# The mixer's sets: high and low parts of the operand side by side, in pairs of PSUM banks

## The chip, the cores and the metric

One core of one Trainium2 chip runs the whole program. The metric is the device time of one execution in microseconds (us). The engines that matter here are TensorE (PE, matmuls; its weight loads are listed apart as PEld), VectorE (DVE), ScalarE (ACT), GpSimd (POOL) and SyncE (SP, which issues most of the loads).

## The reference

One block of a network on 512 positions of width 1024, all in float32: a feed-forward layer (FFN), a mixer, a second FFN, and a last norm.

```
x = x + 0.5 * swiglu(rmsnorm(x), ffn1_w_gu, ffn1_w_down)
x = x + hybrid_mixer(rmsnorm(x), w_in, ...)
x = x + 0.5 * swiglu(rmsnorm(x), ffn2_w_gu, ffn2_w_down)
return rmsnorm(x)

hybrid_mixer(h):
  cb, cc, cu, q, k, v, g_lr, r, ga, gb = split(h @ w_in)
  y_conv = (cb * causal_short_conv(cc * cu)) @ w_out_conv
  log_a  = log_sigmoid(g_lr @ gate_w_up + gate_b) / 16
  o      = chunked gated linear attention of q, k, v, log_a     (4 heads, chunks of 64)
  y_gla  = (rmsnorm(o) * silu(r)) @ w_out_gla
  return (sigmoid(ga) * y_conv + sigmoid(gb) * y_gla) @ w_o
```

The product h @ w_in has a depth of 1024 and more than 8000 columns; it is the mixer's largest piece of work, and the change lies in it.

## The kernel before

**Precision.** Every float32 operand of a matmul is used as a high part (rounded to the matmul's format) and a low part (what the rounding left). A product of weights w and activations a is three matmuls into the same PSUM bank: high w by high a, high w by low a, low w by high a. The high part of a weight tile `wh` is cast on ScalarE (L382), the low part `wl` is the difference, on VectorE (L383), both 128x1024. Three buffers of each are in turn, and the parts are made two steps ahead of their use. Raw weights arrive in tiles `f` by DMAs of SyncE's queue.

**Sets.** Much of the work is done in sets, by a seven-product scheme for 2x2 blocks: the depth is halved, the 512 positions are halved, and two blocks of 256 output columns stand against the two depth halves. In place of eight block products seven are computed, with sums of weight blocks (on VectorE, L367, and by accumulating DMAs on GpSimd's queue, L357) and sums of activation blocks. The products are named m1, p2, q6, p5, q7, p4, p3. One set is 512 output columns by 512 positions at depth 1024, and one product is depth 512 (four tiles, k) by 256 columns (two tiles, e) by 256 positions. The products accumulate into three banks: "b" takes m1, q6, q7 and p4 in turn, with copies of m1, q6 and q7 taken out on ScalarE in between; "a" takes p2; "c" takes p5 and then p3. The quarters of the output are read out of PSUM on VectorE with a kept copy added: p2 + m1, -(c) - q7, c + q6; the last quarter is -b after p4.

**Two forms of a set.** `Set.run` (L563 on) takes an operand whose high and low parts are two tiles. Each (k, e) of a product is three matmuls of 256 positions (all at L577). `run_joint` (L586) takes an operand in which, for each k, 256 high and 256 low values stand side by side. In m1, q6, q7 and p4 it issues the same three matmuls (L607). In p2, p5 and p3 it writes a pair of banks, one bank for each e: one matmul of 512 (L599) multiplies the high weights by high and low part at once, so the main sum comes to stand in the left half of the bank and the cross term in the right half, and one matmul of 256 (L601) adds low weights by high part to the right half. Whoever reads such a bank adds both halves. Before the change the FFNs' sets use the joint form, and the mixer's sets the other.

**The banks.** PSUM has eight banks. Two are the auxiliary ones (`AUX`). The other six are a pool of six single banks (`MM`), or, after `open_banks(True)`, a pool of two single ones and a pool of two pairs (`MM2`). The FFN opens the pairs ahead of its sets and closes them after.

**The mixer's order.** First q and k of the heads by plain products (two heads in a group, then four products `mm_single`, L410 to L412), with `gates(0)` among them. Then v's set (`Tall`, L672 on): the same seven products with the roles exchanged, so that the activations are the stationary operand and 512 weight columns the moving one (L693); it uses two banks for each of "a", "b", "c". Then twelve sets: ga, gb, ga, gb, four of the convolution, two of cb, two of r. The order of products of consecutive sets is woven together by `order`, so that m1 and p2 of the next set come between q7, p4 and p3 of the one before. The steps of the attention are hooks that run after certain products: for each head `gates` (L1171), `decays` (L1186 to L1198), `scale` (L1203), `scores` (L1219), `state`, `output` and `squares`. Head 1's gates come after set 0, head 2's in set 3, head 3's in set 6. `conv_done`, `cb_done` and `act_done` read a set's quarters out of PSUM; `quarter` (L1409) does it for the last two.

**What orders the work.** TensorE takes the products in the order of the plan. Outside the last stage of the program, a planner at compile time places each engine's instructions by the order of the code and by its own reckoning of what is ready; each engine then works through its queue in that order. Pools hand a buffer out again once its last reader is through.

`Operands` makes the summed and split activations of each product when they are needed, two products ahead at the latest: `sum` (L635 to L642) on VectorE, then the cast on ScalarE (L665) and the difference on VectorE (L666), both of 128x1024. In the joint layout it does that in two halves (L658, L659).

Of the kernel before, what the change touches and what calls it, by code (L numbers as in the profile page):

```python
# [12 lines left out]
ALU = mybir.AluOpType  # L13
ENG = mybir.EngineType

P = 128
S = 512
# [62 lines left out]
HW = 256  # L80
# [138 lines left out]
def block_kernel(ctx: ExitStack, tc: tile.TileContext, xT, vecs, gf, gup, wgl, wts, out):  # L219
    nc = tc.nc  # L220
# [8 lines left out]
    def open_banks(pairs):  # L229

        if "ps" in banks_of:
            banks_of["stack"].close()
        banks_of["stack"] = ExitStack()
        banks_of["n"] = banks_of.get("n", 0) + 1
        banks_of["ps"] = banks_of["stack"].enter_context(
            tc.tile_pool(name=f"ps{banks_of['n']}", bufs=2 if pairs else 6,
                         space=bass.MemoryType.PSUM, reuse_waits="tile"))
        if pairs:
            banks_of["pairs"] = banks_of["stack"].enter_context(
                tc.tile_pool(name=f"pp{banks_of['n']}", bufs=2,  # L240
                             space=bass.MemoryType.PSUM, reuse_waits="tile"))
# [16 lines left out]
    def tile_of(pool, shape, dtype=F32):  # L258
        cnt[0] += 1
        return pools[pool].tile(shape, dtype, tag=pool, name=f"{pool}{cnt[0]}")  # L260

    def T(dtype=F32):
        return tile_of("tp", [P, S], dtype)

    def MM():
        cnt[0] += 1
        return banks_of["ps"].tile([P, S], F32, tag="mm", name=f"mm{cnt[0]}")

    def MM2():
        cnt[0] += 1  # L270
        return banks_of["pairs"].tile([P, 2, S], F32, tag="mm2", name=f"mm{cnt[0]}")
# [275 lines left out]
    def mul(out_, a, b, eng=None):  # L547
        (eng or nc.vector).tensor_tensor(out=out_, in0=a, in1=b, op=ALU.mult)  # L548
# [123 lines left out]
    class Tall:  # L672
# [7 lines left out]
        def run(self, p, s):  # L680
            b = {"p2": "a", "p5": "c", "p3": "c"}.get(p, "b")
            fresh = b not in self.bank
            if fresh:
                self.bank[b] = [MM(), MM()]
            bh, bl = self.group.get(p)
            h, l = W.take()
            for i in range(2):
                k = 2 * s + i
                wh, wl = (a[:, 512 * i : 512 * (i + 1)] for a in (h, l))
                for e in range(2):  # L690
                    c = slice(k * HW + e * P, k * HW + (e + 1) * P)
                    for n, (aa, ww) in enumerate(((bh, wh), (bh, wl), (bl, wh))):
                        nc.tensor.matmul(self.bank[b][e], aa[:, c], ww,  # L693
                                         start=fresh and i == 0 and n == 0,
                                         stop=k == 3 and n == 2, skip_group_check=True)
            if s == 1:
                self.done(p, self.bank[b])

    def run_sets(make, ahead=2, hooks={}, tall=None):


        at = W.taken
        seq = []
        while STEPS[at + len(seq)][1] is not None:
            seq.append(STEPS[at + len(seq)])
        sets = {n: None for n, _ in seq if n not in TALL}
        number = {n: i for i, n in enumerate(sets)}
        for n, i in number.items():
            sets[n] = make(i)
        for i, (n, p) in enumerate(seq):  # L710
            for n_, p_ in seq[i : i + ahead + 1]:
                (tall if n_ in TALL else sets[n_]).group.make(p_)
            if n in TALL:
                tall.run(p, TALL[n])
                at = ("tall", TALL[n], p)
            else:
                sets[n].run(p)
                at = (number[n], p)
            for f in hooks.get(at, ()):
                f()  # L720
# [325 lines left out]
    def mixer(norm, nxt):  # L1046
# [21 lines left out]
        def G_tile(i, dtype=F32):  # L1068
# [13 lines left out]
            out=maskf, in_=maskf, pattern=[[1, P]], compare_op=ALU.is_ge, fill=0.0,  # L1082
# [13 lines left out]
        for i in range(2):  # L1096
# [3 lines left out]
                                    in1=gl_w[i][:, :, 0, :RANK].bitcast(F32), op=ALU.subtract)  # L1100
# [3 lines left out]
        for i in range(6):  # L1104
# [3 lines left out]
                                in1=gup_w[R2 : 2 * R2].bitcast(F32), op=ALU.subtract)  # L1108
# [18 lines left out]
        def evac_k(h, o):  # L1127
# [7 lines left out]
                                in1=glr[2 * R2 : R3].bitcast(F32), op=ALU.subtract)  # L1135
# [14 lines left out]
                        in1=row, op0=ALU.mult, op1=ALU.mult)  # L1150
            return X[:, 4 * j : 4 * j + 4, l * HW : (l + 1) * HW]

        xo = Operands(normed)


        def chunks(t):
# [187 lines left out]
        def pair(t):  # L1344
            return t.rearrange("p (e t) -> p e t", t=HW)

        def half(l):
            return slice(l * HW, (l + 1) * HW)
# [19 lines left out]
        def finish_late():  # L1368
            while late:
                late.pop(0)()  # L1370

        def conv_done(i):
            def done(s, p):
                bank, v = s.bank, s.v
                u = Y[i][:, :, 2:]
                if p == "p2":
                    s.t1 = T()
                    nc.vector.tensor_tensor(out=s.t1, in0=bank["a"], in1=v["m1"], op=ALU.add)
                if p == "q7":
                    s.u2 = T()  # L1380
                    nc.vector.scalar_tensor_tensor(out=s.u2, in0=bank["c"], scalar=-1.0,
                                                   in1=v["q7"], op0=ALU.mult, op1=ALU.subtract)
                if p == "p4":
                    nc.vector.scalar_tensor_tensor(
                        out=u[:, :, half(0)], in0=pair(bank["b"]), scalar=-1.0, in1=pair(s.t1),
                        op0=ALU.mult, op1=ALU.mult)
                if p == "p3":
                    t2 = T()
                    nc.vector.tensor_tensor(out=t2, in0=bank["c"], in1=v["q6"], op=ALU.add)
                    mul(u[:, :, half(1)], pair(s.u2), pair(t2))  # L1390
                    late.append(lambda: convolve(i))
            return done
# [16 lines left out]
        def quarter(s, p):  # L1409

            bank, v = s.bank, s.v
            if p not in ("p2", "q7", "p3"):
                return None
            t = T()
            if p == "q7":
                nc.vector.scalar_tensor_tensor(out=t, in0=bank["c"], scalar=-1.0, in1=v["q7"],
                                               op0=ALU.mult, op1=ALU.subtract)
            else:
                nc.vector.tensor_tensor(out=t, in0=bank["a" if p == "p2" else "c"],
                                        in1=v["m1" if p == "p2" else "q6"], op=ALU.add)  # L1420
            return t

        def act_done(func, use):
# [32 lines left out]
        def make(n):  # L1456
# [7 lines left out]

            return Set(xo, done)

        run_sets(make, hooks=hooks, tall=Tall(xo, v_done))
        finish_late()


# [10 lines left out]
        def gate(name, d):  # L1481
            t = T()
            nc.sync.dma_start(t, gates_d[name][d])
            nc.scalar.activation(t, t, AF.Sigmoid)
            return t
# [9 lines left out]
        for d in range(KD):  # L1495
            t = gate("ga", d)
# [12 lines left out]
        for d in range(KD):  # L1509
            t = gate("gb", d)  # L1510
# [87 lines left out]
```

## Time and profile before

| | us |
|---|---|
| median of three runs | 1190.02 (1189.88 to 1190.07) |
| the profiled execution | 1189.97 |
| its span, first to last instruction | 1188.3 |
| TensorE busy in the span | 1177.6 |
| VectorE busy | 900.4 |
| ScalarE busy | 606.5 |
| v's set, about | 391 to 437 |
| the mixer's twelve sets, about | 437 to 707 |

A row of instructions gives start and duration in us, the engine, the line of the kernel, the operation, out<-in by the program's names, the shape, and how many neighbouring instructions were merged into the row; in brackets stands the idle time of the engine before it and whose work ended that. Rows of matmuls overlap, since the next starts before the last has drained; so the distance between starts, not the duration, is what a matmul takes up of TensorE's time.

### The profile page before, as it was taken

The page shows a single profiled execution, that of the slowest core. Times are in us where ns is not written, and L with a number is a line of the kernel's source. Part 1 is how long each engine was busy: PE and PEld are TensorE (multiplying, and loading weights), DVE is VectorE, ACT ScalarE, POOL GpSimd, SP SyncE. Part 2 cuts the span into 40 slices and gives each one's busy share as a digit, 9 for nine tenths or more (in the row PEclk, how much of TensorE's full clock was granted, in tenths as well). Part 3 has the DMA queues.
Part 4 walks back from the last instruction along what each step waited for, and adds up shares of the span by engine and source line. Part 5 has one row for each costly group of instructions (what it writes and reads, how often), then busy time and mean ns, then how long its engine had stood idle before and what let it go on. Part 6 is the DMA issues. An engine that isn't in the chain of part 4 may idle for free. (4 is left out here: it accounts for less than half of the span.)

```text
span 1188.3 us, 18713 instructions
## 1 busy us (share of the span) xinstructions
PE 1177.6 (99%) x7546; PEld 1071.7 (90%) x7546; DVE 900.4 (76%) x1107; ACT 606.5 (51%) x759; POOL 111.3 (9%) x149
## 2 busy tenths in 40 slices
PE   9999999999999999999999999999999999999997
PEld 8899999999988889999999998888889999998886
DVE  7987676989797976677787795455598767785686
ACT  6564555545452847464654564334355554572353
POOL 0011111011110110111010100100001111100100
PEclk9999999999999999999999999999999999999999
DMA  9478787656481776877567766602547777763431
GB/s 350 96 195 186 185 182 192 176 125 164 95 301 60 171 194 175 217 181 199 137 160 163 184 189 192 211 3 98 194 97 189 175 181 182 187 172 116 92 93 71
DMA packets 59335, 193.93 MB, mean 163 GB/s; under 512 B 6672, under 2 KB 10896, under 8 KB 59248
## 3 DMA queue, kind: packets, MB, share of 16 engines
q1 hardware_dynamic: 36912, 124.27, 30.7%
q0 software_dynamic: 17696, 63.97, 29.4%
q10 hardware_dynamic: 4640, 4.49, 1.2%
q8 instruction: 59, 0.97, 0.3%
q14 instruction: 28, 0.23, 0.1%
HBM read 124.55 MB, written 8.39 MB: 112 GB/s over the span
## 5 line engine op out<-in xcount | busy, mean ns | idle before, releaser
L382 ACT CAST wh<-f 128x1024 fp32r<-128x1024 f32 (+1 forms) x331 | 345.9, 1047 | 433.3 <-PE mm L577 123.9
L383 DVE TENSOR_TENSOR wl<-f,wh 128x1024 fp32r<-128x1024 f32 (+1 forms) x331 | 402.3, 1218 | 154.0 <-ACT wh L382 147.1
L577 PE MATMUL mm<-op,wh 128*128 128x256 f32 x1792 | 325.3, 284 | 0.0
L577 PEld LDWEIGHTS mm<-op,wh 128*128 128x128 f32 x1792 | 279.6, 191 | 0.9
L577 PE MATMUL mm<-op,wl 128*128 128x256 f32 x896 | 254.3, 284 | 0.7 <-DVE wl L383 0.7
L607 PE MATMUL mm<-op,wh 128*128 128x256 f32 x1152 | 209.6, 283 | 0.4 <-DVE tp L548 0.4
L357 POOL DMA_DIRECT2D f<-f x114 | 98.3, 863 | 922.4 <-DVE wl L383 489.5
L607 PEld LDWEIGHTS mm<-op,wh 128*128 128x128 f32 x1152 | 179.1, 191 | 2.3 <-issue 0.8
L577 PEld LDWEIGHTS mm<-op,wl 128*128 128x128 f32 x896 | 171.4, 191 | 1.2 <-DVE wl L383 1.1
L607 PE MATMUL mm<-op,wl 128*128 128x256 f32 x576 | 163.0, 283 | 0.0
L599 PE MATMUL mm<-op,wh 128*128 128x512 f32 x432 | 154.4, 398 | 0.0
L601 PE MATMUL mm<-op,wl 128*128 128x256 f32 x432 | 121.3, 281 | 0.0
L410 PE MATMUL mm<-op,wh 128*128 128x512 f32 x292 | 113.7, 389 | 0.0
L412 PE MATMUL mm<-op,wl 128*128 128x512 f32 x292 | 113.6, 389 | 0.0
L411 PE MATMUL mm<-op,wh 128*128 128x512 f32 x292 | 113.6, 389 | 0.0
L607 PEld LDWEIGHTS mm<-op,wl 128*128 128x128 f32 x576 | 110.2, 191 | 0.0
L599 PEld LDWEIGHTS mm<-op,wh 128*128 128x128 f32 x432 | 81.3, 188 | 18.2
L601 PEld LDWEIGHTS mm<-op,wl 128*128 128x128 f32 x432 | 81.7, 189 | 0.0
L410 PEld LDWEIGHTS mm<-op,wh 128*128 128x128 f32 x292 | 54.8, 188 | 11.5 <-issue 0.2
L411 PEld LDWEIGHTS mm<-op,wh 128*128 128x128 f32 x292 | 54.8, 188 | 11.4
L412 PEld LDWEIGHTS mm<-op,wl 128*128 128x128 f32 x292 | 54.8, 188 | 11.4
L434 PE MATMUL mm<-op,wh 128*128 128x512 f32 x256 | 63.8, 391 | 0.0
(266 smaller groups left out, 1455.8 us busy)
## 6 DMA issues: line engine op xcount, KB each, us to landing
f<-wts SPq DMA_DIRECT2D x219, 512.0 KB, 4.4
f<-f POOLq DMA_DIRECT2D x114, 512.0 KB, 4.9
X<-xT SPq DMA_DIRECT2D x8, 256.0 KB, 5.2
xs<-X POOLq DMA_DIRECT2D x8, 256.0 KB, 4.6
ga<-tp ACTq DMA_DIRECT2D x8, 256.0 KB, 5.1
gb<-tp ACTq DMA_DIRECT2D x8, 256.0 KB, 4.5
tp<-ga SPq DMA_DIRECT2D x8, 256.0 KB, 6.1
tp<-gb SPq DMA_DIRECT2D x8, 256.0 KB, 2.7
```

The lines of the kernel that those rows point to most:

```text
L357: nc.gpsimd.dma_start(out_, a, accum_op=ALU.add)
L382: nc.scalar.copy(h[:, :w], raw[:, :w])
L383: nc.vector.tensor_tensor(out=l[:, :w], in0=raw[:, :w], in1=h[:, :w].bitcast(F32), op=ALU.subtract)
L410: nc.tensor.matmul(o, wh, ah, start=first, stop=False)
L411: nc.tensor.matmul(o, wh, al, start=False, stop=False)
L412: nc.tensor.matmul(o, wl, ah, start=False, stop=last)
L434: nc.tensor.matmul(o[c], w[:, s : s + P], a[k], start=k == 0 and j == 0, stop=k == kt - 1 and j == 2)
L577: nc.tensor.matmul(to, ww[:, s], aa[:, t], start=fresh and k == 0 and e == 0 and j == 0, stop=k == 3 and j == 2, skip_group_check=True)
L599: nc.tensor.matmul(o[:, e], h[:, s], a, start=fresh and k == 0, stop=False, skip_group_check=True)
L601: nc.tensor.matmul(o[:, e, HW:], l[:, s], a[:, :HW], start=False, stop=k == 3, skip_group_check=True)
L607: nc.tensor.matmul(to, ww[:, s], aa, start=fresh and k == 0 and e == 0 and j == 0, stop=k == 3 and j == 2, skip_group_check=True)
```

## The change

The mixer's operand `xo` is made in the joint layout, so the mixer's twelve sets run through `run_joint`: p2, p5 and p3 become 512-wide and 256-wide matmuls into pairs of banks. The pairs are opened ahead of v's set and closed after the last set. v's set takes its stationary 128 columns, high and low, from the new layout, and takes "b" and "c" as pairs of banks and "a" as two single ones. `quarter` reads the left halves with the kept copy and then adds (or, for q7, subtracts) the right halves in a second VectorE instruction, and `conv_done` now calls `quarter` in place of its own three copies of that code.

```diff
         def run(self, p, s):
             b = {"p2": "a", "p5": "c", "p3": "c"}.get(p, "b")
             fresh = b not in self.bank
-            if fresh:
+            if fresh and b == "a":
                 self.bank[b] = [MM(), MM()]
-            bh, bl = self.group.get(p)
+            elif fresh:
+                two_banks = MM2()
+                self.bank[b] = [two_banks[:, e] for e in range(2)]
+            parts = self.group.get(p)
             h, l = W.take()
             for i in range(2):
                 k = 2 * s + i
                 wh, wl = (a[:, 512 * i : 512 * (i + 1)] for a in (h, l))
                 for e in range(2):
-                    c = slice(k * HW + e * P, k * HW + (e + 1) * P)
+                    bh, bl = (parts[k // 2][:, k % 2 * S + o : k % 2 * S + o + P]
+                              for o in (e * P, HW + e * P))
                     for n, (aa, ww) in enumerate(((bh, wh), (bh, wl), (bl, wh))):
-                        nc.tensor.matmul(self.bank[b][e], aa[:, c], ww,
+                        nc.tensor.matmul(self.bank[b][e], aa, ww,
...
-        xo = Operands(normed)
+        xo = Operands(normed, joint=True)
...
                 if p == "p2":
-                    s.t1 = T()
-                    nc.vector.tensor_tensor(out=s.t1, in0=bank["a"], in1=v["m1"], op=ALU.add)
+                    s.t1 = quarter(s, p)
                 if p == "q7":
-                    s.u2 = T()
-                    nc.vector.scalar_tensor_tensor(out=s.u2, in0=bank["c"], scalar=-1.0,
-                                                   in1=v["q7"], op0=ALU.mult, op1=ALU.subtract)
+                    s.u2 = quarter(s, p)
...
                 if p == "p3":
-                    t2 = T()
-                    nc.vector.tensor_tensor(out=t2, in0=bank["c"], in1=v["q6"], op=ALU.add)
+                    t2 = quarter(s, p)
...
             t = T()
+            bank = bank["a" if p == "p2" else "c"]
+            main, cross = bank[:, :, :HW], bank[:, :, HW:]
             if p == "q7":
-                nc.vector.scalar_tensor_tensor(out=t, in0=bank["c"], scalar=-1.0, in1=v["q7"],
-                                               op0=ALU.mult, op1=ALU.subtract)
+                nc.vector.scalar_tensor_tensor(out=pair(t), in0=main, scalar=-1.0,
+                                               in1=pair(v["q7"]), op0=ALU.mult, op1=ALU.subtract)
             else:
-                nc.vector.tensor_tensor(out=t, in0=bank["a" if p == "p2" else "c"],
-                                        in1=v["m1" if p == "p2" else "q6"], op=ALU.add)
+                nc.vector.tensor_tensor(out=pair(t), in0=main,
+                                        in1=pair(v["m1" if p == "p2" else "q6"]), op=ALU.add)
+            nc.vector.tensor_tensor(out=pair(t), in0=pair(t), in1=cross,
+                                    op=ALU.subtract if p == "q7" else ALU.add)
             return t
...
+        open_banks(True)
         run_sets(make, hooks=hooks, tall=Tall(xo, v_done))
+        open_banks(False)
         finish_late()
```

## The prediction

> **What bounds the kernel now.** I read the page's busy table first, then the busy time by stage, then TensorE's own waits, and last the rows in order of time, where the pitch of the matmuls and the lateness of the weight splits can be read.
>
> ```profile
> span 1188.3 us, 18713 instructions
> PE 1177.6 (99%) x7546; PEld 1071.7 (90%) x7546; DVE 900.4 (76%) x1107; ACT 606.5 (51%) x759; POOL 111.3 (9%) x149
> ```
>
> ```profile
> 391.00:437.00 46.00, 46.00 (x225) 38.19 (x224) 39.85 (x46) 29.41 (x38) 6.00 (x7) 1.00 0.77 180
> 437.00:707.00 270.00, 268.79 (x2189) 264.32 (x2188) 203.44 (x254) 154.30 (x200) 27.94 (x36) 1.00 0.70 177
> 85.00:110.00 25.00, 25.00 (x189) 23.89 (x188) 18.52 (x20) 12.94 (x16) 3.44 (x4) 1.00 0.79 185
> ```
>
> The second fence is busy time by stretch (us, then PE, weight load, VectorE, ScalarE, GpSimd, clock, DMA share, GB/s). v's set runs in 391 to 437, the mixer's twelve sets in 437 to 707; the third row lies in the first FFN's sets, which already have the layout that the change brings. TensorE is busy throughout at full clock, so the kernel's time is the sum of matmul pitches plus the few stalls. TensorE's waits, whole kernel:
>
> ```profile
> PE mm L577 <- DVE wl L383: 0.7, 2, 0.6
> PE aux L1225 <- DVE qk L548: 0.5, 1, 0.5
> PE mm L607 <- DVE tp L548: 0.4, 1, 0.4
> ```
>
> All three end on VectorE, and the first two are in the mixer's sets. So two things decide: what the new matmul mix costs in pitch, and what more VectorE work does to these waits.
>
> **The change part by part.** The profiled execution took 1189.97 us (span 1188.3 and 1.7 around it), the median of the runs is 1190.02; the sum is made against 1189.97.
>
> *Matmuls.* A product p2, p5 or p3 of a set has 8 pairs (k, e) of three 256-wide matmuls. Afterwards each pair is one 512-wide and one 256-wide matmul. Busy time misleads here (a 512-wide row lasts 0.40, a 256-wide 0.28, by which the pair would save a fifth): rows overlap, and starts count. In the first FFN:
>
> ```profile
> 99.02 0.40 PE L599 MATMUL mm<-op,wh 128*128 128x512 f32 x1
> ...
> 101.83 0.40 PE L607 MATMUL mm<-op,wh 128*128 128x256 f32 x2
> ...
> 110.47 0.40 PE L599 MATMUL mm<-op,wh 128*128 128x512 f32 x1
> ```
>
> From 99.02 to 101.83 runs one joint product: 2.81 us. From 101.83 to 110.47 run three products of 24 narrow matmuls: 8.64, so 2.88 each, 0.12 a matmul. A whole FFN set, from one first reading (below) at 93.52 to the next at 113.50, takes 19.98; seven narrow products would take 20.16. That is 0.06 for each joint product, against 0.07 by the single one. The mixer's twelve sets have 36: 36 x 0.06 = 2.2 us saved (up to 2.5). The weight loads saved (288) cost nothing of their own: they run beside matmuls. v's set keeps its 168 matmuls of 512; only the address of their stationary operand changes: nothing.
>
> Here the TensorE page of the Trainium skill (TensorE: Matmul & The Clock Gate, section Back-to-back issue gap) speaks against the change: it gives a warm gap of N/2.4 + 2.5 ns, so 109 ns for 256 and 216 for 512. By it three narrow ones (327.5) and the pair (325) differ by 2.5 ns, 288 of them make 0.7 us, and the sum below would be 1191.7. The trace does not agree: 120 ns for 256, and the pair, 353, saves 7; the measurement decides.
>
> *Second reading of each pair of banks.* p2, q7 and p3 of a set now need two VectorE instructions where one did. The FFN's sets show the price:
>
> ```profile
> 93.52 0.69 DVE L787 TENSOR_TENSOR tp<-mm,tp 128x512 f32<-128x512 f32 x1 [0.53 <-PE mm L601]
> ...
> 113.50 0.69 DVE L787 TENSOR_TENSOR tp<-mm,tp 128x512 f32<-128x512 f32 x1 [0.53 <-PE mm L601]
> 114.23 0.69 DVE L790 TENSOR_TENSOR tp<-tp,mm 128x512 f32<-128x512 f32 x1
> 114.83 1.22 DVE L383 TENSOR_TENSOR wl<-f,wh 128x1024 fp32r<-128x1024 f32 x1
> ```
>
> One reading moves the queue by 0.60 (114.23 to 114.83), two by 1.33: 0.73 more, 36 times, 26.3 us on VectorE. It goes from 203.4 of 270 to about 230, 85%: not the bound on the mean. Behind a second reading wait the weight splits (L383), which TensorE needs a product or two later. An ordinary one:
>
> ```profile
> 520.19 1.23 DVE L383 TENSOR_TENSOR wl<-f,wh 128x1024 fp32r<-128x1024 f32 x1 [1.94 <-ACT wh L382]
> ```
>
> ```profile
> 525.22 0.28 PE L577 MATMUL mm<-op,wl 128*128 128x256 f32 x1
> ```
>
> It has 1.94 us of idle time before it and ends 3.8 before its first use: that hides 0.73. If the cover is gone, each second reading costs its 0.73. It is gone where a head's gates and decays share the queue, so I look for stretches without idle time and for the splits at their end:
>
> ```profile
> 468.53 0.69 DVE L1182 TENSOR_TENSOR g<-g,g 128x512 f32<-128x512 f32 x1 [1.30 <-ACT g L1181]
> 476.40 0.69 DVE L1416 SCALAR_TENSOR_TENSOR tp<-mm,tp 128x512 f32<-128x512 f32 x1
> 478.08 1.22 DVE L383 TENSOR_TENSOR wl<-f,wh 128x1024 fp32r<-128x1024 f32 x1
> ```
>
> ```profile
> 479.35 0.38 PE L577 MATMUL mm<-op,wl 128*128 128x256 f32 x1 [0.15 <-DVE wl L383]
> ```
>
> Stretch A (head 1): the idle 1.30, an ACT result's, absorbs what is added earlier; after it one reading, then the split for which TensorE waits already. Its second reading goes straight through: 0.73.
>
> ```profile
> 526.71 0.69 DVE L1182 TENSOR_TENSOR g<-g,g 128x512 f32<-128x512 f32 x1 [1.20 <-ACT g L1181]
> 532.57 0.68 DVE L1378 TENSOR_TENSOR tp<-mm,tp 128x512 f32<-128x512 f32 x1
> 535.50 0.68 DVE L1419 TENSOR_TENSOR tp<-mm,tp 128x512 f32<-128x512 f32 x1
> 539.92 2.35 DVE L383 TENSOR_TENSOR wl<-f,wh 128x1024 fp32r<-128x1024 f32 x2
> ```
>
> ```profile
> 542.50 0.28 PE L577 MATMUL mm<-op,wl 128*128 128x256 f32 x1
> ```
>
> Stretch B (head 2): two readings, 1.46, ahead of a split that ends at 541.14 and is needed at 542.50, 1.36 in hand: 0.1.
>
> ```profile
> 591.74 0.69 DVE L1182 TENSOR_TENSOR g<-g,g 128x512 f32<-128x512 f32 x1 [1.14 <-ACT g L1181]
> 594.62 0.67 DVE L1381 SCALAR_TENSOR_TENSOR tp<-mm,tp 128x512 f32<-128x512 f32 x1
> 596.40 2.36 DVE L383 TENSOR_TENSOR wl<-f,wh 128x1024 fp32r<-128x1024 f32 x2
> 601.54 0.69 DVE L1378 TENSOR_TENSOR tp<-mm,tp 128x512 f32<-128x512 f32 x1
> 604.21 0.69 DVE L1389 TENSOR_TENSOR tp<-mm,tp 128x512 f32<-128x512 f32 x1
> 606.41 0.69 DVE L548 TENSOR_TENSOR qk<-g,qk 128x512 f32<-128x512 f32 x1
> ```
>
> ```profile
> 597.67 0.38 PE L577 MATMUL mm<-op,wl 128*128 128x256 f32 x1 [0.58 <-DVE wl L383]
> 607.16 0.49 PE L1225 MATMUL aux<-qk 128*128 128x128 f32 x2 [0.48 <-DVE qk L548]
> ```
>
> Stretch C (head 3): one reading before the split at 596.40, for which TensorE already waits: 0.73. Two more before the scaling of k, for which the scores (L1225) wait: up to 1.46 more. But the planner sets the scores among the matmuls of p5 where it reckons them ready (they break into a product), so they can slip behind matmuls at no cost: between 0 and 1.46, I take half, 0.73.
>
> *Splitting the operands in halves.* Each of seven products of the operand is now cast and subtracted in two pieces of 512. The subtraction in one piece moves the queue from 395.13 to 396.26, by 1.13; two pieces at 0.60 make 1.20: 0.07 each. ScalarE's two casts cost about as much more and it is 64% busy there.
>
> ```profile
> 394.55 0.67 DVE L548 TENSOR_TENSOR qk<-mm,row 128x512 f32<-128x512 f32 x1
> 395.13 1.22 DVE L666 TENSOR_TENSOR op<-X,op 128x1024 fp32r<-128x1024 f32 x1
> 396.26 1.22 DVE L383 TENSOR_TENSOR wl<-f,wh 128x1024 fp32r<-128x1024 f32 x1
> ```
>
> VectorE has no idle time here, and TensorE already waits a little for the split at 396.26:
>
> ```profile
> 397.54 0.50 PE L693 MATMUL mm<-wl,op 128*128 128x512 f32 x1
> ```
>
> This row starts 0.08 later than the pitch of 0.23 would have it and lasts 0.11 longer. One operand's halves lie ahead of it: 0.1 in all.
>
> *Banks.* Opening the pairs closes the pool of six, and the first matmul on a reopened bank waits for that bank's last reader. In the first FFN this is the third wait above, 0.4. In the mixer the last bank before v's set is read only at 394.55 to 395.22, though v's first matmul starts at 391.79; only if that very bank lies in v's first pair does it cost, 3.4 us. I take 0, since one late bank among six is not likely among the two needed, and p2's banks come 5 us later; bound 3.4. Closing the pairs after the sets comes in the FFN too, and the list of TensorE's waits has none there.
>
> ```profile
> 391.79 0.39 PE L693 MATMUL mm<-wh,op 128*128 128x512 f32 x1
> ```
>
> The sum: 1189.97 - 2.2 + 0.73 (A) + 0.1 (B) + 0.73 + 0.73 (C) + 0.1 = 1190.2. By the bounds of C and of the saving it lies between 1189.1 and 1190.9. No step is moved, and the loads of SyncE's and GpSimd's queues are issued at the same products as before.
>
> **The rivals.**
> All hidden: the planner orders VectorE's queue anew and no second reading reaches TensorE. Then 1189.97 - 2.2 = 1187.8; only if the old waits (1.2) go too is it 1186.6. Against it: in A and C nothing is idle that could give way.
> The other side, VectorE becomes the bound around the heads: the planner puts a head's work ahead of the splits, so that in A, B and C all three second readings of a set reach TensorE. 3 x 2.2 - 2.2 = 4.4: 1194.4. It decides from the point where a stretch of 20 us has no idle time; A to C last 10 to 18. Against: most splits follow idle time.
> The opening wait of 3.4 comes: 1193.6.
> p5 waits for a pair: if it takes the bank pair of the set before, set 4's p5 needs the reading at 535.50, pushed by 1.46 and ended at 537.65, but it started at
>
> ```profile
> 536.50 0.40 PE L577 MATMUL mm<-op,wh 128*128 128x256 f32 x2
> ```
>
> so 1.15 more: 1191.3. Against: in the FFN no joint matmul is in the list of waits, and the pair of its own p2 is read earlier (532.57).
> The saving is smaller: were the mixer's pair of matmuls 0.3575 in place of the 0.353 that the set's pitch gives (2.82 over eight), three narrow ones being 0.36, 0.7 would be left, and 1191.7. Against: the rows from 99 to 110. This is what the page's formula would come to.
>
> **How the numbers follow.** Forecast 0.60, p5's wait 0.10, all hidden 0.08, old waits gone too 0.04, small saving 0.02, VectorE bound 0.10, opening wait 0.06. What a measurement here tells from no change is 0.2%, 2.4 us: 1187.6 to 1192.4. Faster holds only the 0.04, slower the last two, 0.16, the rest is the same, 0.80. The range runs from all hidden, 1187.7, to 1192.8, short of the last two.
>
> **What would show it.** Right: L599 and L601 with 288 more each, L577 with 2016 fewer; joint products of 2.81 to 2.82 in the mixer; TensorE's waits on L383 near 479 and 597 longer by about 0.7; VectorE near 230 in the sets. Wrong: waits of L693 on L548 at 392 (opening), waits on second readings before p5, or splits late in stretches that are idle now.

## The result and the profile after

| | us | ratio to before, 95% interval |
|---|---|---|
| before, median of 7 | 1190.07 (1189.59 to 1190.55) | |
| after, median of 7 | 1193.65 (1192.96 to 1194.96) | 1.0031 [1.0022, 1.0041] |
| the profiled execution after | 1193.44, span 1191.7 | |

The change costs 3.6 us. The forecast was 1190.2, and the time lies above the end of its range, 1192.8. The page of after, busy us of the span, and busy time by stretch (us, then PE, weight load, VectorE, ScalarE, GpSimd, clock, DMA share, GB/s):

```profile
span 1191.7 us, 18199 instructions
PE 1176.6 (99%) x7258; PEld 1054.6 (88%) x7258; DVE 921.3 (77%) x1150; ACT 608.3 (51%) x766; POOL 111.4 (9%) x149
```

```profile
391.00:437.00 46.00, 44.73 (x212) 36.04 (x211) 39.39 (x51) 28.22 (x40) 6.00 (x7) 1.00 0.74 175
437.00:709.00 272.00, 269.06 (x1913) 250.03 (x1912) 220.71 (x286) 156.01 (x202) 28.01 (x36) 1.00 0.70 176
```

TensorE has 288 matmuls fewer and is busy 1.0 us less, at the same full clock, and yet the span is 3.4 longer: it waits more. In v's set alone its busy time goes down from 46.00 of 46.00 to 44.73. TensorE's waits in after (total us, times, longest), those from v's set on that before does not have:

```profile
PE mm L601 <- DVE wl L383: 1.7, 2, 1.2
PE mm L697 <- DVE wl L383: 1.3, 2, 1.1
PE mm L607 <- DVE wl L383: 1.2, 2, 0.6
...
PE aux L931 <- DVE wl L383: 0.4, 1, 0.4
PE mm L412 <- DVE wl L383: 0.4, 1, 0.4
```

All are for `wl`, the low part of a weight. L697 is v's set, L601 and L607 are the mixer's sets, L412 is in the plain products behind them (726.63), and L931 is in the last stage (1071.54). Cut into stages at starts of matmuls in the trace (v's set from its first to its last matmul; from there to the end of the twelve sets; from there to the last matmul of the second FFN's sets; from there to the last matmul), the us of the two profiled executions are:

| | v's set | twelve sets | to FFN2's last set | rest |
|---|---|---|---|---|
| before | 43.99 | 271.34 | 359.17 | 115.12 |
| after | 46.11 | 271.42 | 359.91 | 115.67 |
| difference | +2.12 | +0.08 | +0.74 | +0.55 |

So the twelve sets, where the forecast looked for everything, come out even. The 3.6 us are mostly v's set, and then two places behind the sets.

**The sets.** A joint product in the mixer, rows of TensorE in after (start, duration):

```profile
659.00 0.40 PE L599 MATMUL mm<-op,wh 128*128 128x512 f32 x1
659.23 0.28 PE L601 MATMUL mm<-op,wl 128*128 128x256 f32 x1
...
660.73 0.40 PE L607 MATMUL mm<-op,wh 128*128 128x256 f32 x2
```

Five pairs take 1.73, 0.346 each, here. Over all twelve sets, from start to start and without the steps that end in a wait, 288 pairs take about 0.357 each where three narrow matmuls took 0.363: 1.7 us saved. Experiment 1 below gives 2.1. The rows of the new waits there:

```profile
475.92 0.39 PE L607 MATMUL mm<-op,wl 128*128 128x256 f32 x1 [0.61 <-DVE wl L383]
...
482.92 0.39 PE L601 MATMUL mm<-op,wl 128*128 128x256 f32 x1 [0.54 <-DVE wl L383]
...
545.79 0.39 PE L607 MATMUL mm<-op,wl 128*128 128x256 f32 x1 [0.62 <-DVE wl L383]
...
601.96 0.38 PE L601 MATMUL mm<-op,wl 128*128 128x256 f32 x1 [1.18 <-DVE wl L383]
```

They make 2.95 us of idle time, and the waits of before (0.15, 0.58 and 0.48) are gone or in them: 1.74 more. The fourth stands in place of two.

**v's set.** The long wait there, in after's TensorE, VectorE and ScalarE:

```profile
404.60 0.50 PE L697 MATMUL mm<-wl,op 128*128 128x512 f32 x1 [1.09 <-DVE wl L383]
404.93 0.63 PE L697 MATMUL mm<-wh,op 128*128 128x512 f32 x2
```

```profile
402.12 0.68 DVE L659 TENSOR_TENSOR op<-X,op 128x512 fp32r<-128x512 f32 x1
402.72 0.68 DVE L548 TENSOR_TENSOR y<-g,y 128x512 f32<-128x512 f32 x1
403.33 1.22 DVE L383 TENSOR_TENSOR wl<-f,wh 128x1024 fp32r<-128x1024 f32 x1
```

```profile
398.69 1.14 ACT L658 CAST op<-X 128x512 fp32r<-128x512 f32 x2 [2.52 <-DVE X L637]
399.74 0.62 ACT L1200 ACTIVATE g<-g 128x512 f32<-128x512 f32 x1
400.27 0.60 ACT L658 CAST op<-X 128x512 fp32r<-128x512 f32 x1
400.78 1.07 ACT L1301 ACTIVATE y<-mm 128x512 f32<-128x512 f32 x2
401.75 1.04 ACT L382 CAST wh<-f 128x1024 fp32r<-128x1024 f32 x1
```

The weight of step 4 of v's set is split by the cast at 401.75 and the difference at 403.33. In before the same two stand here, on ScalarE and on VectorE:

```profile
396.75 0.60 ACT L1297 ACTIVATE y<-mm 128x512 f32<-128x512 f32 x1 [0.64 <-PE mm L693]
398.65 1.06 ACT L665 CAST op<-X 128x1024 fp32r<-128x1024 f32 x1 [1.30 <-DVE X L637]
399.61 0.59 ACT L1297 ACTIVATE y<-mm 128x512 f32<-128x512 f32 x1
400.09 1.05 ACT L382 CAST wh<-f 128x1024 fp32r<-128x1024 f32 x1
```

```profile
401.40 1.22 DVE L383 TENSOR_TENSOR wl<-f,wh 128x1024 fp32r<-128x1024 f32 x1
```

Before, ScalarE takes out m1's first bank at 396.75, in time in which it has nothing else, and the second right after the operand's cast. Afterwards both evictions stand together behind that cast (which waits 2.52 for VectorE's sum), behind an exponential of the decays (L1200) and behind half of the next operand's cast. The weight cast comes 1.66 later, its low part 1.93 later. TensorE is through with what it has at 403.5.

### The profile page after: what moved, and what is told of

Read it like the earlier page. It is cut to its first block, busy times and chain, and to the rows that moved or that the text cites. A ratio compares the mean times of both kernels' runs of the same rounds, so it can differ in the third digit from the quotient of the medians.

```text
span 1191.7 us, 18199 instructions
## 1 busy us (share of the span) xinstructions
PE 1176.6 (99%) x7258; PEld 1054.6 (88%) x7258; DVE 921.3 (77%) x1150; ACT 608.3 (51%) x766; POOL 111.4 (9%) x149
## 5 line engine op out<-in xcount | busy, mean ns | idle before, releaser
L607 PE MATMUL mm<-op,wh 128*128 128x256 f32 x1920 | 350.7, 284 | 0.4 <-DVE tp L548 0.4
L607 PEld LDWEIGHTS mm<-op,wh 128*128 128x128 f32 x1920 | 298.7, 191 | 3.7 <-issue 0.8
L607 PE MATMUL mm<-op,wl 128*128 128x256 f32 x960 | 271.9, 283 | 1.2 <-DVE wl L383 1.2
L599 PE MATMUL mm<-op,wh 128*128 128x512 f32 x720 | 258.0, 399 | 0.0
L601 PE MATMUL mm<-op,wl 128*128 128x256 f32 x720 | 202.6, 282 | 1.7 <-DVE wl L383 1.7
L607 PEld LDWEIGHTS mm<-op,wl 128*128 128x128 f32 x960 | 183.5, 191 | 1.8 <-DVE wl L383 1.6
L599 PEld LDWEIGHTS mm<-op,wh 128*128 128x128 f32 x720 | 135.4, 188 | 30.0 <-ACT tp L611 0.2
L601 PEld LDWEIGHTS mm<-op,wl 128*128 128x128 f32 x720 | 136.1, 189 | 2.6 <-DVE wl L383 2.2
L412 PE MATMUL mm<-op,wl 128*128 128x512 f32 x292 | 113.7, 389 | 0.4 <-DVE wl L383 0.4
L410 PE MATMUL mm<-op,wh 128*128 128x512 f32 x292 | 113.6, 389 | 0.0
L411 PE MATMUL mm<-op,wh 128*128 128x512 f32 x292 | 113.6, 389 | 0.0
L577 PE MATMUL mm<-op,wh 128*128 128x256 f32 x448 | 80.7, 283 | 0.0
L577 PEld LDWEIGHTS mm<-op,wh 128*128 128x128 f32 x448 | 70.0, 192 | 0.1
L412 PEld LDWEIGHTS mm<-op,wl 128*128 128x128 f32 x292 | 54.8, 188 | 12.1 <-DVE wl L383 0.8
L410 PEld LDWEIGHTS mm<-op,wh 128*128 128x128 f32 x292 | 54.8, 188 | 11.6 <-issue 0.2
L411 PEld LDWEIGHTS mm<-op,wh 128*128 128x128 f32 x292 | 54.8, 188 | 11.4
L434 PE MATMUL mm<-op,wh 128*128 128x512 f32 x256 | 63.6, 390 | 0.6 <-DVE op L485 0.6
L434 PEld LDWEIGHTS mm<-op,wh 128*128 128x128 f32 x256 | 48.0, 188 | 11.0 <-ACT acc L494 0.8
```

The lines of the kernel that those rows point to most:

```text
L410: nc.tensor.matmul(o, wh, ah, start=first, stop=False)
L411: nc.tensor.matmul(o, wh, al, start=False, stop=False)
L412: nc.tensor.matmul(o, wl, ah, start=False, stop=last)
L434: nc.tensor.matmul(o[c], w[:, s : s + P], a[k], start=k == 0 and j == 0, stop=k == kt - 1 and j == 2)
L577: nc.tensor.matmul(to, ww[:, s], aa[:, t], start=fresh and k == 0 and e == 0 and j == 0, stop=k == 3 and j == 2, skip_group_check=True)
L599: nc.tensor.matmul(o[:, e], h[:, s], a, start=fresh and k == 0, stop=False, skip_group_check=True)
```

## The experiments

Theory at the start: the second readings cost about what they save (D). Three rivals for v's set, where the forecast had 0.1: the halved operand work (H), the pairs of banks (P), and later the order of the queues (O) against the banks themselves (B). Ratios are against runs of before on the same chip.

**1. Without the second readings.** The cross terms of p2, p5 and p3 are left out of the result.

```diff
-            nc.vector.tensor_tensor(out=pair(t), in0=pair(t), in1=cross,
-                                    op=ALU.subtract if p == "q7" else ALU.add)
             return t
```

> The changed kernel without the second reading in the mixer's quarters (36 VectorE instructions of 0.69 us; the cross terms are left out of the result of these quarters). Theory D: the new waits in the twelve sets and just after them (0.77 and 0.69 at 476 and 483, 0.78 at 546, 0.55 at 727, above what the kernel before had there) come from the second readings: they go, about 2.5 us, and the time is near 1191. v's set still takes 46.1 us from its first to its last matmul. Rival: these waits come from the new banks or another order of the queue, and stay: 1193.6.

Measured: 1190.14 us (1189.48 to 1190.68), ratio 1.0 [0.999, 1.0009]. v's set 46.13, the sets 269.02, then 359.15 and 115.23. So without the second readings the sets gain 271.34 - 269.02 = 2.32 us; 0.2 of that are shorter waits (1.00 us in place of 1.21), and 2.1 the joint products. With the second readings 3.5 of the whole go: 2.40 in the sets, 0.76 after them and 0.44 in the last stage, though the last does not hang on the readings (see what stays open). v's set does not move, so its 2.1 have another cause.

**2. The operand's work in one piece.** One cast and one difference of the whole operand, in tiles of 2048, the layout still the joint one.

```diff
-                t = [tile_of("op", [P, 1024], F32R) for _ in range(2)]
-                for i in range(2):
-                    a = t[i].rearrange("p (k b t) -> p k b t", b=2, t=HW)
-                    vi = v[:, 2 * i : 2 * i + 2]
+                two = tile_of("op", [P, 2048], F32R)
+                t = two[:, :1024], two[:, 1024:]
+                n = 4 if self.whole else 2
+                for i in range(0, 4, n):
+                    a = two.rearrange("p (k b t) -> p k b t", b=2, t=HW)[:, i : i + n]
+                    vi = v[:, i : i + n]
```

> The changed kernel with the mixer's operand cast and subtracted in one piece of 1024 again (its two tiles are one of 2048, so that one instruction reaches both; all operand tiles are taken in such twos, the FFNs' operand is still made in halves). Theory H: the 2.1 us that v's set has lost (44.0 to 46.1 from first to last matmul) come from the halves: v's set is back near 44.1 and the time near 1191.5. Theory P: they come from the pairs of banks in v's set, whose readings start only when both banks are done: v's set stays at 46.1, time 1193.6.

Measured: 1192.85 (1192.5 to 1193.46), 1.0022 [1.0013, 1.0031]; v's set 46.00. The halves are not it. The edit also takes all other operand tiles in twos, and in its profile v's set starts 1.1 later (392.85 against 391.76). The stage after the sets is 359.39 here, 0.2 above before, although all the second readings are in.

**3. Halves alone, on the kernel before.** The separate high and low tiles are kept and made in two pieces each; nothing else is changed.

```diff
-            nc.scalar.copy(hv, v)
-            nc.vector.tensor_tensor(out=lv, in0=v, in1=hv.bitcast(F32), op=ALU.subtract)
+            n = 2 if self.split else 4
+            for i in range(0, 4, n):
+                j = slice(i, i + n)
+                nc.scalar.copy(hv[:, j], v[:, j])
+                nc.vector.tensor_tensor(out=lv[:, j], in0=v[:, j], in1=hv[:, j].bitcast(F32),
+                                        op=ALU.subtract)
```

> The kernel before with one part of the change alone: the mixer's operand is cast and subtracted in two halves each, layout, matmuls and banks as before. Theory H: v's set goes from 44.0 to about 46 us, time 1192. Theory P: v's set stays at 44.0, time 1190.1.

Measured: 1190.23 (1189.73 to 1190.63), 0.9999 [0.999, 1.0008]; v's set 44.03. H falls from this side too: "0.1 in all" is right for the halves.

**4. Pairs of banks alone, on the kernel before.** Pairs opened and closed as in after; v's "b" and "c" are pairs, and the sets' "a" and "c" take the first bank of a pair; all products stay narrow and are read once.

```diff
-                self.bank[b] = MM()
+                self.bank[b] = MM2()[:, 0] if paired[0] and b != "b" else MM()
...
-            if fresh:
+            if fresh and b == "a":
                 self.bank[b] = [MM(), MM()]
+            elif fresh:
+                two_banks = MM2()
+                self.bank[b] = [two_banks[:, e] for e in range(2)]
```

> The kernel before with another part alone: pairs of banks are opened around v's set and the twelve sets, v's set takes two of its three as pairs, the sets use one bank of each pair; operand, matmuls and readings as before. Theory P: v's set goes from 44.0 to about 46 us, time 1192. Theory H: v's set stays near 44.0 and the time at 1190.1.

Measured: 1192.28 (1191.87 to 1192.67), 1.0018 [1.0009, 1.0026]; v's set 46.05, the sets 271.32, 359.17 and 115.15. The 2.1 us of v's set come with the pairs and with nothing else of the change. The rows of ScalarE, VectorE and TensorE:

```profile
401.69 1.07 ACT L1301 ACTIVATE y<-mm 128x512 f32<-128x512 f32 x2
402.65 1.05 ACT L383 CAST wh<-f 128x1024 fp32r<-128x1024 f32 x1
```

```profile
404.36 1.22 DVE L384 TENSOR_TENSOR wl<-f,wh 128x1024 fp32r<-128x1024 f32 x1
```

```profile
405.64 0.53 PE L697 MATMUL mm<-wl,op 128*128 128x512 f32 x1 [1.38 <-DVE wl L384]
```

TensorE does not wait for a bank. It waits for a weight's low part, which is late as in after.

**5. The order on ScalarE.** After, with three edges of order and no other change.

```diff
-                    nc.scalar.copy(a[:, :, 0], vi)
+                    with tc.issue_after(self.behind[p]()) if p in self.behind else nullcontext():
+                        nc.scalar.copy(a[:, :, 0], vi)
...
+            with tc.issue_after(W.casts[ats[0] + 4]):
                 nc.scalar.activation(EX, M, AF.Exp, scale=1.0 / TAU)
                 nc.scalar.activation(M, M, AF.Exp, scale=-1.0 / TAU)
                 nc.scalar.activation(KS, KS, AF.Exp, scale=1.0 / TAU)
...
+        xo.behind = {"q6": lambda: evicted[0], "q7": lambda: W.casts[ats[0] + 5]}
```

> The kernel after, with three orders of issue fixed on ScalarE in v's set and nothing else changed: the cast of q6's operand stands behind the first eviction of m1 (it stood ahead of both), the cast of q7's operand and the three large exponentials of the decays stand behind the weight casts of steps 4 and 5 (they stood ahead of step 4's). The banks stay pairs. Theory O (the pairs cost their 2.1 us only because the planner, seeing both evictions come ready together, put 2 to 3 casts and exponentials ahead of the weight cast that TensorE waits for): v's set back from 46.1 to about 44.1 us, the time from 1193.6 to about 1191.6. Rival B (the pair tile itself holds TensorE: the matmuls to the second bank wait for the reading of the first): v's set stays at 46.1, the time at 1193.6. Between, about 45: part of the order was mended, and another instruction is late next.

Measured: 1193.83 (1193.08 to 1194.33), 1.0031 [1.0019, 1.0043]; v's set 45.61. The 0.5 that v's set gains is its second wait (0.18 at 415.96), which is gone; the long one stays, at 1.13. The time does not fall, since the stage after the sets has grown to 360.93 (by the profiled execution, the slowest of the six). ScalarE has the order that the edges ask for, and TensorE still waits. Rows of ScalarE, VectorE and TensorE:

```profile
397.72 1.09 ACT L1309 ACTIVATE y<-mm 128x512 f32<-128x512 f32 x2 [1.23 <-PE mm L700]
399.01 1.15 ACT L661 CAST op<-X 128x512 fp32r<-128x512 f32 x2 [0.20 <-DVE X L639]
400.06 2.00 ACT L383 CAST wh<-f 128x1024 fp32r<-128x1024 f32 x2
```

```profile
400.63 0.69 DVE L1200 TENSOR_TENSOR g<-g 128x512 f32<-128x512 f32 x1
401.23 0.16 DVE L549 TENSOR_TENSOR d<-sm 128x4 f32<-128x4 f32 x1
401.31 1.22 DVE L644 SCALAR_TENSOR_TENSOR X<-X 128x1024 f32<-128x1024 f32 x1
402.44 1.29 DVE L662 TENSOR_TENSOR op<-X,op 128x512 fp32r<-128x512 f32 x2
403.64 2.36 DVE L384 TENSOR_TENSOR wl<-f,wh 128x1024 fp32r<-128x1024 f32 x2
```

```profile
404.92 0.50 PE L700 MATMUL mm<-wl,op 128*128 128x512 f32 x1 [1.13 <-DVE wl L384]
```

The cast is back at 400.06 (400.09 in before). Now VectorE has new work ahead of the low part: the decays' second difference (L1200) and p4's sum (L644), which in before is done long after, at 417.95. Theory O as it was put, ScalarE's queue alone, is wrong; whether it is VectorE's queue next or the bank is open after this run.

**6. "b" in single banks.** After, with "a" of v's set in a pair in place of "b", and no edges.

```diff
-            if fresh and b == "a":
+            if fresh and b == "b":
                 self.bank[b] = [MM(), MM()]
```

> The kernel after, but in v's set the accumulator b (m1, q6, q7, p4) lies in two single banks again and a (p2) in a pair; no order is fixed. Planned, one operand cast of 0.60 us then leaves the front of step 4's weight cast, while the exponential of 0.62 us stays ahead of it. Theory O (it is the place of the weight cast in ScalarE's queue): v's set mends in part only, by about 0.6 of the 2.1 us, to about 45.5, time about 1193.0. Rival B (the pair tile of b itself): mended wholly, 44.1 and 1191.5.

Measured: 1193.39 (1192.49 to 1194.03), 1.0026 [1.0016, 1.0036]. Here the first set's m1, whose 24 matmuls elsewhere stand ahead of v's last product, comes behind it, so only the sum of v's set and the sets compares: 317.25, after 317.53, before 315.33. TensorE waits 0.51 and 0.31 in v's set, after 1.09 and 0.18. The mend is 0.3 in place of O's 0.6, and B's 2.1 did not come: the banks of "b" as such are not the cause. "c" is a pair here as in after, and "a" has become one, so this run alone does not clear the pairs.

**7. Edges, and half of the places wide.** The edges of experiment 5; sets 1, 2, 4, 6, 7 and 11 go back to three narrow products and one reading.

```diff
-            two_banks = b != "b"
+            two_banks = b != "b" and getattr(self, "wide", True)
...
+            if not s.wide:
+                return t
             nc.vector.tensor_tensor(out=pair(t), in0=pair(t), in1=cross,
...
+            s.wide = n not in (1, 2, 4, 6, 7, 11)
```

> The order of e6_order, and wide products with their second readings in only 18 of the 36 places: in the sets numbered 1, 2, 4, 6, 7 and 11 (those near the heads' work, and the last) p2, p5 and p3 are three narrow products each again, read once. Theory D (a second reading costs only where VectorE is full or the end of the chain waits for it): v's set 44.1, half the 2.3 us saved kept with no new wait in the sets (270.2 from v's set to the end of the sets, 271.3 before), the 0.75 us after the sets gone: 1190.1 - 1.15 = 1188.9, up to 1189.4 if the 0.4 at the end of the second feed-forward stays. Rival (a second reading costs its 0.06 us or more of TensorE time wherever it stands): 271.3 in the sets, 1190.1 or above.

Measured: 1191.31 (1190.56 to 1193.67), 1.0012 [1.0004, 1.0021]. The 1188.9 to 1189.4 was missed, for the most part by v's set: 45.61 (44.1 was expected). But the sets are 270.00 (270.2 expected) and the stage after them is 359.17 (the 0.75 gone, as expected). Theory D holds where it could be tested: 18 places away from the heads' work cost no more than the scores' wait, 1.04 in place of 0.48.

**8. Edges, no second readings.** The edges of experiment 5 in the kernel of experiment 1, with the same cross terms left out.

> The order of e6_order without the 36 second readings (the products with the low part of the operand are then left out of p2, p5 and p3). If v's set's 2.1 us and the sets' saving of 2.3 us are independent, it gives e1_no_second's 1190.1 less 2.0: 1188.1, with v's set at 44.1 and the sets at 269.0. If the order costs elsewhere, up to 1190.

Measured: 1189.63 (1189.03 to 1190.36), 0.9996 [0.9988, 1.0005]; v's set 45.61, the sets 268.88. The order was mended by 0.5 us only, and 0.5 is what it gives against experiment 1; the 1188.1 was missed for the reason seen in experiment 5.

**9. Both orders.** Experiment 5 with VectorE's order too.

```diff
+            with tc.issue_after(W.lows[ats[0] + 4]):
                 nc.vector.tensor_tensor(out=chunks(KS),
...
+                    with tc.issue_after(self.late()) if self.late else nullcontext():
                         nc.vector.scalar_tensor_tensor(out=v, in0=b(0, 0), scalar=-1.0, in1=v,
...
+        xo.late = lambda: W.lows[ats[0] + 5]
```

> e6_order with VectorE's order around the same weight fixed as well, the banks still pairs: the second subtraction of the decays stands behind step 4's weight subtraction, and p4's sum (1.22 us) behind step 5's; in e6_order both stood ahead and step 4's low part began at 403.64 (403.33 in after, 401.40 in before; TensorE asked for it at 403.5). Theory O, in its wider form (the pairs cost through the place of step 4's high and low part in the queues of ScalarE and VectorE, not through the banks): the low part begins near 401.9 and ends before TensorE asks, v's set falls from 45.6 to 44.0-44.2 us, the time to about 1191.6. Rival B (the pair tile itself): v's set stays at 45.6 or above with TensorE's wait moved to another releaser, time 1193.6.

Measured: 1191.96 (1191.09 to 1193.22), 1.0017 [1.0008, 1.0026]; v's set 44.18, against 43.99 in before. VectorE and TensorE at that place:

```profile
400.99 1.28 DVE L666 TENSOR_TENSOR op<-X,op 128x512 fp32r<-128x512 f32 x2
402.20 2.35 DVE L385 TENSOR_TENSOR wl<-f,wh 128x1024 fp32r<-128x1024 f32 x2
```

```profile
403.46 0.62 PE L704 MATMUL mm<-wh,op 128*128 128x512 f32 x2
403.92 0.39 PE L704 MATMUL mm<-wl,op 128*128 128x512 f32 x1
404.14 0.62 PE L704 MATMUL mm<-wh,op 128*128 128x512 f32 x2
```

The wait is gone, and the banks are still pairs. So O in its wider form holds: the pairs cost 2.1 us through the places of one weight's split in two queues, and five edges of order take back 1.9 of it. B falls. Counted from v's first matmul (392.37 here, 391.79 in before), the low part even begins 0.2 later than in before (402.20 against 401.40) and is still in time, since TensorE asks for it at 403.92: how many us it is late is not the price, only what passes the moment at which TensorE asks is. The median falls by 1.7 against after. The stages do not add up to that: in the profiles v's set falls by 1.93 and the stage after the sets grows from 359.91 to 360.99. The profiled execution is the slowest of the eleven (1193.22), so 360.99 is likely more than the median execution has.

**10. and 11. Both orders, and 18 or 21 places wide.** Experiment 7 with experiment 9's edges, and then with set 2 wide as well (narrow in sets 1, 4, 6, 7 and 11).

> e8_order_half with VectorE's order fixed as in e10_both_orders. Theory D with O: v's set 44.1, 270.0 in the sets, 359.2 after them: e8_order_half's 1191.3 less 1.6 = 1189.7, down to 1190.1 - 1.3 = 1188.8 by the stages against before. If the order mends v's set but costs in the first sets: 1190.5 or more.

> e11_both_half with set 2 wide as well (21 of 36 places). Theory D: the waits near 476 and 483 come from the readings of the sets 0 and 1, so set 2 gives its 0.19 us: 269.8 in the sets, time 0.2 under e11_both_half. If set 2's readings make the wait for the scores or the state there: 270.3 or more, and no gain.

Measured: 1189.97 (1189.06 to 1192.17), 1.0003 [0.9994, 1.0012], and 1189.07 (1188.51 to 1190.51), 0.9993 [0.9984, 1.0002]. Stages: 44.19, 270.17, 359.17, 115.41, and 44.18, 269.85, 359.18, 115.13. Of the waits of after in the sets, only one of 0.15 is left, as in before; the scores' wait has grown:

```profile
PE aux L1240 <- DVE qk L551: 1.0, 1, 1.0
```

Set 2 gave 0.32 in the stage, where 0.19 was expected. The 21 places wide are the fastest version here, by 1.0 us against before, but its interval still takes in no change.

**12. The last set narrow, alone.** Experiment 9, with set 11 back to narrow products and one reading; 33 places wide.

> e10_both_orders with the last set alone (number 11) narrow in p2, p5 and p3 and read once; the other 33 places are wide and read twice. Theory E (the wait after the sets comes from the last set's own second readings: its last silu comes late, and the feed-forward's first weights are put behind the work that waits for it): the stage from the end of the sets to the second feed-forward's last set falls from 360.99 to 359.2 us, the sets stay at 271.4 to 271.5, the time falls by 1.8 to about 1190.2. Rival (it is the sum of delays from all the sets): the stage stays above 360.5 and the time at 1191.9.

Measured: 1190.73 (1190.41 to 1191.26), 1.0006 [0.9997, 1.0015]. Stages 44.17, 271.57, 359.17, 115.08. Without the last set's second readings the whole wait after the sets is gone: theory E. The median falls by 1.2, less than the 1.8 of the stage, which is taken against experiment 9's slowest execution. Its way in after, on VectorE, ScalarE and TensorE:

```profile
713.32 0.68 DVE L1423 TENSOR_TENSOR tp<-tp,mm 128x512 f32<-128x512 f32 x1
...
725.36 1.22 DVE L383 TENSOR_TENSOR wl<-f,wh 128x1024 fp32r<-128x1024 f32 x1
```

```profile
714.03 0.63 ACT L1438 ACTIVATE tp<-tp 128x512 f32<-128x512 f32 x1 [3.56 <-DVE tp L1423]
714.69 1.28 ACT L1490 ACT_TABLE_LOAD   x1
...
723.31 1.05 ACT L382 CAST wh<-f 128x1024 fp32r<-128x1024 f32 x1
```

```profile
726.63 0.50 PE L412 MATMUL mm<-op,wl 128*128 128x512 f32 x1 [0.39 <-DVE wl L383]
```

The last quarter's second reading holds back the last silu, and ScalarE waits 3.56 us for it; the sigmoids of the gates and their table stand behind the silu, and the weight casts behind these. The sigmoids wait for loads of ga as well: the last before the cast at 723.31 for 0.85 us, and for 1.50 in experiment 9's profile, where TensorE's wait is 1.23 in place of 0.39. ScalarE makes no weight cast between 709.42 and 723.31, where before had two, at 715.53 and 719.51.

## Why the prediction was wrong

**Matmuls: right.** 2.2 us were forecast; 1.7 come by the rows of after, 2.1 by experiment 1. The rival of a smaller saving (0.7) did not come. It is what the formula gives that the prediction took from the Trainium skill (TensorE: Matmul & The Clock Gate, section Back-to-back issue gap); that section calls it the gap of an isolated matmul. Here a pair saves 6 to 7 ns, not 2.5: the measurement stands. L599 and L601 have their 288 more each, and TensorE 288 instructions fewer.

**v's set: the step that failed.** "Only the address of their stationary operand changes: nothing" left out that its banks change too. Of the banks the prediction asked one question, whether the first matmul waits for the pool that closes: it took 0 there with a bound of 3.4, and that was right, v's set starts at 391.76 as before without a wait. It did not ask what the planner does when two evictions that were released one by one become one bank pair's. The runs put 2.1 us in its place (experiment 4), more than half of the 3.6, and show its way: not the bank, but the place of one weight's cast and difference in ScalarE's and VectorE's queues (experiment 9). The prediction had a hint in hand and used it for 0.1: "VectorE has no idle time here, and TensorE already waits a little". Why the planner orders so differently was not tested; experiment 6, with "b" in single banks, still has much of that order.

**Splitting in halves: right**, 0.1 and no more (experiments 2 and 3).

**Second readings: right in the sets' sum, by luck, wrong in place, and one place missed.** Forecast were 2.3 us in A, B and C; the sets lost 2.4 by experiment 1. The sum agrees only because A and B came out too small and C too large. The price on VectorE was too high: its busy time grew by 20.9 us in the whole program, not by 26.3, and to 220.71 in the sets, not to about 230. The 1.33 for two readings holds where one follows straight on the other; in after that is so 14 times of 36, elsewhere other work stands between them and the second moves the queue by about 0.60.
- A, forecast 0.73: two waits, 0.61 and 0.54, where there was one of 0.15: 1.0. That the idle 1.30 "absorbs what is added earlier" is wrong. After it, the gates' difference (L1186) came at 471.45, 2.92 later than in before, 0.8 more than v's set's delay. The idle time was for a result of ScalarE, and ScalarE had itself waited for a second reading, whose result its own queue stores first. In before, and in experiment 1, the table load in this place does not wait; store and table load of ScalarE in after:

```profile
469.09 0.37 ACTq L1445 DMA_DIRECT2D ga<-tp  x1
469.49 1.28 ACT L1185 ACT_TABLE_LOAD   x1 [1.04 <-DVE tp L1423]
```

- B, forecast 0.1: 0.62. The 1.36 us in hand were measured on the old TensorE. The new one comes earlier by what it saved: 545.17 without the wait, less 437.87 where v's set ends and less some 1.2 more than in before lost in A, is 106.1 us into the sets, against 542.50 - 435.78 = 106.7 in before. The saving itself used up nearly half of the slack.
- C, forecast 1.46: 1.18 in one wait in place of 0.58 and 0.48: 0.1. The scores' own wait is gone; half of their 1.46 was taken.
- After the sets: nothing was forecast, 0.74 came. It goes with the last set's readings (experiment 12), though experiment 2 has them and loses only 0.2. The prediction looked for splits late in the sets, and stopped at their end, where the silu of the last quarter stands in a chain.

Of the rivals, "VectorE becomes the bound around the heads" (1194.4) comes nearest in time but not in its cause: VectorE is busy 220.71 of 272 there, and the sets stayed even. "p5 waits for a pair" did not come; no wait of L599 is in the list. The prediction's list of TensorE's waits in the whole kernel shows three of five; the other two, 1.1 us each at L284 and L910, are the same in after.

**Open.** The last stage takes 0.55 us more in after. Experiment 8 has it without any second reading (115.66) and experiment 2 does not have it with all of them (115.09), so it hangs neither on the readings nor on the layout alone. In the trace it is TensorE's wait at 1071.54 for a low part, and ahead of that ScalarE waits longer for the load of a raw weight than in before (1.27, at 1059.93):

```profile
1063.39 1.05 ACT L382 CAST wh<-f 128x1024 fp32r<-128x1024 f32 x1 [1.88 <-DMA f<-f]
```

In the five profiles in which this cast waits some 1.9 us or more for its load, TensorE then waits 0.4 to 0.5; where it waits about 1.3 for it, TensorE waits 0.1 at most. Experiment 2 does not fit in: 1.67 there, and TensorE does not wait for this low part. Why the load lands late in some of them was not settled. In the sets, the saving of 1.7 by after's rows and of 2.1 by experiment 1 differ by 0.4, of which one wait more, beyond its idle time (last section), would be 0.26.

## What to carry to other kernels

Where a planner orders the queues, a change of how tiles are grouped (two banks in one tile) can move work that nobody touched: for each tile whose grouping changes, find the weight or operand split that TensorE needs next, and how many us it has in hand. A saving on TensorE uses up that slack as surely as more work on VectorE does, so both belong in the same subtraction. And a chain that ends a stage deserves the same look as the stage: here the last set's readings alone cost 1.2 us by the medians of the experiments 9 and 12, and between 0.2 and 1.8 by single profiles.

## What was not expected of the hardware

A wait costs TensorE more than the idle time that the row shows, by 0.26 to 0.27 us here. At 404.60 in after the idle time is 1.09, but this start comes 1.48 after the one before it and the next 0.33 after that, in place of 0.23 each: 1.35 lost. At 415.96 it is 0.18 idle and 0.44 lost. The first part is that the row before lasts on after the next could have started (0.39 long, 0.23 apart: 0.16; the ends of matmul rows are modelled by the profile, the starts are not). The second is that the first matmul after the wait takes 0.33 to the next start in place of 0.23. In the 256-wide stream it is the same:

```profile
476.14 0.40 PE L607 MATMUL mm<-op,wh 128*128 128x256 f32 x2
```

The start at 475.92 comes 0.89 after the one before, and this one 0.22 after it, in place of 0.12 each: 0.87 lost with 0.61 idle. A forecast that adds up idle times in brackets is short by that much for each new wait.
